# A hybrid encoder on one core: the order of every engine's instructions, written down as tables

## The chip, the core and the metric

The kernel runs on one core of one Trainium2 chip. A core has five engines that run side by side, each through its own queue in order: TensorE (PE in the profile; its weight loads are shown apart, as PEld), VectorE (DVE), ScalarE (ACT), GpSimd (POOL) and SyncE (SP). In this kernel SP issues most of the DMAs, POOL the rest, among them DMAs that add onto a tile in SBUF. An instruction that must wait for another engine holds up all that stand behind it in its own queue.

The metric is the device time of one execution in microseconds (us), the median of several runs.

## The reference

Two post-norm residual layers over 512 tokens of width 1024, in float32. Layer 0 mixes tokens by a bidirectional gated DeltaNet (8 heads of 128, a short convolution on q, k and v), layer 1 by a bidirectional GLA (4 heads, keys of 128, values of 256, a gate for each key channel). Each mixer is followed by a squared-ReLU MLP of 4096, and each of these four parts by `LayerNorm(alpha * x + part(x))`. Cut to what matters:

```python
def reference(x, ...):
    for i in range(DEPTH):                       # DEPTH = 2
        if i % 2 == 0: m = _mixer_gdn(x, ...)    # projections, conv, chunked delta rule both ways, rmsnorm * silu(z), w_out
        else:          m = _mixer_gla(x, ...)    # projections, gates, chunked GLA both ways, rmsnorm * silu(r), w_out
        x = _layernorm(DEEPNORM_ALPHA * x + m, ln1_g[i], ln1_b[i])
        a = relu(x @ mlp_w1[i])
        x = _layernorm(DEEPNORM_ALPHA * x + (a * a) @ mlp_w2[i], ln2_g[i], ln2_b[i])
    return x
```

## The kernel before

**Products in three parts.** Every large product runs on pairs of numbers in the `float32r` type: ACT rounds an operand to a high part (`nc.scalar.copy`, L104), DVE subtracts that from the operand for the low part (L105), and `mm3` (L130 to L136) issues three matmuls, high by high (L133), high by low and low by high (L135, L136). So each block of weights costs a DMA into a staging buffer (`wst`, four of them), a cast on ACT and a subtraction on DVE before PE can use it, and the staging buffer is free for the next load when both are done. The split parts go to `wh` and `wl` (three buffers each), in the MLPs also to `w2h`, `w2l` (three) and `ah`, `al` (two).

**Stages.** In the profiled execution: the DeltaNet layer from 0 to about 417 us (`gdn`), the first MLP to about 757 (`mlp`), GLA to about 976 (`gla`), and the second MLP to the end. In DeltaNet each head goes through generators (`project`, `rows`, `solve`, `recur`, `attend`, `finish`): long projections in `mm3` (PE tiles `pjq`, `pjk`, `pjv`, `pjz`), between them small fp16 groups of the triangular solve (`lv`, `hp`, `nw`) and fp32 groups of the recurrence (`m1`, `m2`, `m3`, `op`). The gates of all heads come once at the start (`gates`; `gcp` at L1492 is their cumulated sum). In the MLPs, products over half the tokens and half the depth are combined Strassen-like: `pq` (256 wide) are the first products, `pX`, `pY`, `pZ` (512 wide) the second ones, `pl` the last group. In GLA, score groups (`scp`), states (`stp`), outputs (`op`), value products (`pjv`) and the output projection (`oa`) alternate; weights of the value products are combined by adding DMAs that POOL issues (`ch<-wst`, L1068).

**What sets the order.** A scheduler (the Tile layer) orders each engine's instructions by the dependences and a priority that follows the program text; `high_priority` raises some. Inside `with c.in_order(engine)` (L61) it may not: there each instruction of that engine gets an order-only dependence on the one ahead of it in the text. This holds for PE in the start of DeltaNet, in both MLPs, in GLA and in GLA's last projection, for POOL in the MLPs and DeltaNet's constants, and for ACT in one loop of the MLPs. There the author's interleaving in the text is the order; elsewhere, and on DVE and SP throughout, it is the scheduler's.

Of the kernel before, what the change touches and what calls it, by code (L numbers as in the profile page):

```python
# [28 lines left out]
class Ctx:  # L29
# [23 lines left out]
    def after(self, ins, before):  # L53

        self.tc.add_manual_dep(
            ins.ins, before.ins.name, mybir.DependencyInfo(mybir.DependencyClass.Sync, mybir.DependencyReason.DATA),
            reason="paced")
        return ins

    @contextlib.contextmanager  # L60
    def in_order(self, engine):  # L61
# [267 lines left out]
    def out_last(self, w, ks, lhs, z, tags, par, homes=None, xtags=("tp",), late=0, room=None):  # L329

        nc = self.nc
        homes = iter(homes or [None] * len(ks))
        ws = [[self.wrows(w, k * P, hf * 512, next(homes)) for k in ks[::2]] for hf in range(2)]
        banks = {}
        self.cols = room and (par, room)

        def part(t, hf, js):
            sl = slice(t * P, (t + 1) * P)
            if (t, hf) not in banks:
                banks[t, hf] = self.bank([P, 512], F32, name="ob", tag=tags[(2 * t + hf) % len(tags)])  # L340
                if not room:
                    nc.tensor.matmul(banks[t, hf], self.ident, z[t][hf], start=True, stop=False)
            for i in js:
                ah, al = lhs(ks[i], sl)
                wh, wl = ws[hf][i // 2]
                self.mm3(banks[t, hf], ah, al, wh[:, i % 2, :], wl[:, i % 2, :], room is not None and i == 0, i == len(ks) - 1)

        n, m = len(ks), len(ks) // 2
        with self.in_order(mybir.EngineType.PE) if late else contextlib.nullcontext():
            if late:  # L350
                for t in range(2):
                    for hf in range(2):
                        part(t, hf, range(m))
            for t in range(NT):
                for hf in range(2):
                    part(t, hf, range(m if late and t < 2 else 0, n))
                    if hf == 0 and 0 < late <= t:
                        self.xpose(t - late, self.xt[t - late], xtags)
                    if room:
                        nc.vector.tensor_tensor(self.xh(t)[hf], z[t][hf], banks[t, hf], ALU.add)  # L360
                if room:
                    self.whiten(self.xh(t))
                else:
                    self.layernorm([banks[t, hf] for hf in range(2)], self.xh(t), par, last=late and t == NT - 1)
                if not late:
                    self.xpose(t, self.xt[t], xtags)
        return [t for t in range(NT - late, NT)]


def mlp(c, w1, w2, g, b, left, before=None, out=None):  # L370
# [13 lines left out]
    with c.banks(pj=2, X=2, Y=2, Z=2), tc.tile_pool(name="mlp", bufs=2) as pool:  # L384
# [372 lines left out]
        for j, t in enumerate(left):  # L757
            for q, run in enumerate(c.xposes(t, "Y", "Z")):
                between[(2, 4 * q) if j == len(left) - 1 else (0, 4 + 3 * q)] = run
        with c.in_order(mybir.EngineType.PE), c.in_order(mybir.EngineType.Pool):  # L760
            hs = {0: h}
            tail = last(G - 1, hs)
            units = seconds(hs, tail)
            halves = c.proj_halves(specs, between)
            for f, ps in enumerate(halves):
                done = act(ps, h[0][:, f, :])
                load_part(0, 0, f // 2, f % 2, done if f > 1 else None)
                if f == 0 and before:
                    lnp.extend(c.load_ln(*before, ln_tile(), acts[0]))
                    c.cols = None  # L770
            combo = combos()
            def run(n):
                for _ in range(n):
                    next(combo, None)
            op = next(combo)
            work = pairs(op, hs)
            run(3)
            w = c.wcols(w1, GF // 2 * P)
            for f in range(4, GF):
                nw = c.wcols(w1, (f + 1) * P) if f + 1 < GF else None  # L780
                run(1 if f == 6 else 2)
                done = feature(f, h, w)
                w = nw
                if f in (4, 5):
                    load_part(0, 1, 1, f % 2, done)
                if f == 5:
                    load(0, 1, 0, acts[-1])
                if f == 6:
                    next(units)
                    next(work)  # L790
            not_done.clear()
            for _ in combo:
                pass
            with c.in_order(mybir.EngineType.Activation):
                for _ in work:
                    next(units)
                next(units, None)
            par.extend(c.load_ln(g, b, ln_tile(), acts[-1]))
            for _ in tail:
                pass  # L800


def load_x(c, x, tags, zero):
    c.new_xt()
    c.new_x()
    for t in range(NT):
        c.dma(c.xt[t], x[t * P:(t + 1) * P, :])
    idle = c.bank([P, S], F32, name="idle", tag="pj")

    def warm(n=1):  # L810
        for _ in range(n):
            c.nc.tensor.matmul(idle, zero[:, 0, :], zero[:, 0:NT, :], start=True, stop=True)

    with c.in_order(mybir.EngineType.PE):
        warm(7)
        c.marks = [c.xpose(t, c.xt[t], tags, warm=warm if t < NT - 1 else None) for t in range(NT)]
    return c.marks[-1]
# [52 lines left out]
def gla(c, gc, w_in, gate_w2, w_out, cols):  # L870
# [5 lines left out]
    with c.banks(ac=2, tp=2, X=2, Y=2), tc.tile_pool(name="gla", bufs=2) as pool, \  # L876
# [11 lines left out]
        c.dma(gst, w_in[:, base:base + 32].rearrange("(k p) n -> p k n", p=P))  # L888
        specs = [(c.stack(gst, 3), "gps", "ac")]
        specs += [(c.wcols(w_in, c0), nm, "XY"[nm == "pjk"]) for c0, nm in ((0, "pjq"), (H * P, "pjk"))]  # L890
        with c.in_order(mybir.EngineType.PE):
            gps, *qk0 = c.proj_halves(specs, dict(zip(((2, 0), (2, 4)), c.xposes(NT - 1, "tp", "tp"))))
        low = slice(64, 96)
        gl3 = pool.tile([P, S], F32R, name="gl3", tag="gl3", bufs=1)
# [19 lines left out]
        lhs = lambda k, sl: tuple(t[:, k % 4, sl] for t in o_pair(k // 4))  # L914
        early = list(range(KT // 2))
        vr = GlaValues(c, pool, w_in, heads)
        with c.in_order(mybir.EngineType.PE):
            list(heads[0].qk(qk0))
            heads[0].gates(0)
            heads[0].gates(1)  # L920
            def stream():
                yield from heads[1].qk()
                yield from vr.products(0)
                yield from heads[2].qk()
                yield from vr.products(2)
                yield from heads[3].qk()
                c.new_xt()
                for t in range(NT):
                    c.dma(c.xt[t], kept[t * P:(t + 1) * P, :])
                    z.append(c.xh(t))  # L930
                yield from c.out_pieces(w_out, early, lhs, z, ("X", "Y"))

            work = stream()

            def behind(n):
                for _ in range(n):
                    next(work, None)

            spare = pool.tile([P, NT, 2 * B_DV], F32, name="vs", tag="vs", bufs=3)
            vr.first = vr.combos(spare)  # L940
            level = heads[0].levels()
            next(level)
            for _ in range(2):
                next(vr.first)
            behind(10)
            after = None
            for h in range(H):
                for s in level:
                    behind(FILL[h].get(s, 0))
                    if s == NORM_AT and after:  # L950
                        after()
                    if s in (16, 32) and h + 1 < H:
                        heads[h + 1].gates(s // 32)
                level = heads[h + 1].levels() if h + 1 < H else iter(())
                steps = iter(STEPS[h])

                def beside():
                    units, levels = next(steps)
                    behind(units)
                    for _ in range(levels):  # L960
                        next(level, None)

                heads[h].states(beside)
                after = heads[h].norm
            behind(2)
            after()
            behind(99)
# [12 lines left out]
class GlaValues:  # L980


    ORDER = (1,2,5,6,7,4,3)
# [352 lines left out]
class GdnConst:  # L1336


    def __init__(self, c, pool, pz, w_in, a_log, dt_bias, conv_w, norm_g, behind):
# [11 lines left out]
        V.memset(self.eps[:, 1:2], math.log(0.5 * P * RMS_EPS))  # L1351
        self.ng = pool.tile([P, 1], F32, name="ng", bufs=1)
        self.cw = pool.tile([P, 5, 24], F32, name="cw", bufs=1)
        with c.in_order(mybir.EngineType.Pool):
            self.gates(w_in, a_log, dt_bias, conv_w, norm_g, behind)
            self.masks()

# [63 lines left out]
    def gates(self, w_in, a_log, dt_bias, conv_w, norm_g, behind):  # L1421
# [29 lines left out]
            nc.tensor.transpose(ps[:, :120], cw, c.ident[:120, :120])  # L1451
            V.tensor_copy(self.cw, ps[:, :120].rearrange("p (k t) -> p k t", k=5))

        with c.in_order(mybir.EngineType.PE):
            ps, self.k0 = c.proj_halves([(ws, "bap", "ch"), (k0, "pjk", "ac")], {(1, 6): taps})
        yr = pool.tile([2 * M, S], F32, name="yr", tag="E", bufs=2)
        nc.scalar.copy(yr, ps[:2 * M, :])
# [501 lines left out]
        "b_gate_b", "b_norm_g", "b_w_out", "ln1_g", "ln1_b", "mlp_w1", "mlp_w2", "ln2_g", "ln2_b"]  # L1959


def body(tc, nc, a, out):
    with contextlib.ExitStack() as es:
        def pool(name, bufs, **kw):
# [4 lines left out]
        with tc.tile_pool(name="gcst", bufs=1) as gp:  # L1969
# [5 lines left out]
            left = gla(c, gc, a["b_w_in"][0], a["b_gate_w2"][0], a["b_w_out"][0], cols)  # L1975
        mlp(c, a["mlp_w1"][1], a["mlp_w2"][1], a["ln2_g"][1], a["ln2_b"][1], left,
            (a["ln1_g"][1], a["ln1_b"][1]), out=out[0])


# [16 lines left out]
```

## Time and profile before

| | |
|---|---|
| three runs | 1339.14, 1340.04, 1342.2 us; median 1340.04 |
| profiled execution | 1339.26 us, of which span 1337.6 |
| busy: PE, PEld, DVE, ACT, POOL | 1312.5, 1127.9, 1127.6, 777.7, 118.8 us |
| matmul records | 8726 |
| busy PE by stage (0:417, 417:757, 757:976, 976:1337.6) | 410.3, 338.0, 212.3, 352.0 us |

How to read it: times are microseconds from the span's start. A row of the timeline has the start, the length, the engine, the line, the operation and out<-in by the program's names, and in brackets how long the engine stood idle ahead of it and what ended that. A row of the waits names who waited for whom, then the total, the count and the longest one. The chain of waits follows the work that ended last backwards, at each step to what released it. A row by groups has the busy time and the mean in ns. Matmuls are pipelined, and the ends of their records are modelled. A row by stretch of time has, after the stretch, its length and then the busy time of PE, PEld, DVE, ACT and POOL with the number of instructions, the granted clock, the share of the DMA engines and GB/s.

### The profile page before, as it was taken

What the parts mean: (1) busy time and instruction counts of PE and PEld (TensorE: products, weight loads), DVE (VectorE), ACT (ScalarE), POOL (GpSimd) and SP (SyncE); (2) the same over time, 40 slices, a digit from 0 to 9 for tenths busy, and PEclk for the clock granted to TensorE, in tenths of its full rate; (3) what the DMA queues carried; (4) which work ended last, traced back from release to release, by engine and by line L of the source; (5) the groups of instructions that cost most, each with busy time, mean ns of one, the idle gap of its engine ahead of it and who ended that gap; (6) DMA issues with size and microseconds to landing.
All of it is one profiled execution on the core that took longest, in us unless ns stands there. A gap on an engine that the chain in (4) does not pass through costs nothing.

```text
span 1337.6 us, 22200 instructions
## 1 busy us (share of the span) xinstructions
PE 1312.5 (98%) x8726; PEld 1127.9 (84%) x8726; DVE 1127.6 (84%) x1738; ACT 777.7 (58%) x1477; POOL 118.8 (9%) x180
## 2 busy tenths in 40 slices
PE   8999999999999999999999999999999999999997
PEld 7778887888888899999998878877879899999986
DVE  6798898998768897988977889888877998889875
ACT  4766667666534656656563358647357556566640
POOL 6600000000001000101001011110000001001000
PEclk9999999999999999999999999999999999999999
DMA  7321111211133765556521666464125665556411
GB/s 196 79 64 49 49 49 48 64 46 47 52 111 110 196 135 152 130 160 160 124 83 63 183 140 158 101 152 126 44 68 156 176 173 145 139 156 129 126 63 48
DMA packets 155289, 148.86 MB, mean 111 GB/s; under 512 B 7425, under 2 KB 124193, under 8 KB 155184
## 3 DMA queue, kind: packets, MB, share of 16 engines
q1 hardware_dynamic: 144416, 115.62, 29.2%
q0 software_dynamic: 10624, 31.55, 12.6%
q8 instruction: 68, 1.11, 0.3%
q14 instruction: 37, 0.30, 0.1%
q10 hardware_dynamic: 144, 0.26, 0.1%
HBM read 118.06 MB, written 4.19 MB: 91 GB/s over the span
## 4 chain that ended last, share of the span: by engine, by line
PE 82%; DVE 7%; ACT 5%; DMA 3%; issue 2%; SPq 0%; POOL 0%; DVEq 0%; ACTq 0%; POOLq 0%
PE pq L136 6%; PE pq L133 6%; PE pq L135 6%; PE pX L135 3%; PE pX L136 3%; PE pX L133 3%; PE pjv L133 2%; PE pjv L135 2%; PE pjv L136 2%; PE pl L136 2%; PE pl L133 2%; PE pl L135 2%; PE op L1926 2%; PE lv L1789 2%; PE pY L135 2%; PE pY L136 2%
## 5 line engine op out<-in xcount | busy, mean ns | idle before, releaser
L104 ACT CAST wh<-wst 128x1024 fp32r<-128x1024 f32 (+1 forms) x175 | 173.2, 994 | 134.9 <-DVE wst L485 47.5
L105 DVE TENSOR_TENSOR wl<-wst,wh 128x1024 fp32r<-128x1024 f32 (+1 forms) x175 | 201.4, 1153 | 24.7 <-ACT wh L104 23.7
L105 DVE TENSOR_TENSOR w2l<-w2r,w2h 128x1024 fp32r<-128x1024 f32 x84 | 102.6, 1221 | 25.5 <-ACT w2h L104 25.2
L136 PE MATMUL pq<-xth,wl 128*128 128x256 f32 x384 | 108.5, 283 | 0.0
L133 PE MATMUL pq<-xth,wh 128*128 128x256 f32 x384 | 108.5, 283 | 0.0
L135 PE MATMUL pq<-xtl,wh 128*128 128x256 f32 x384 | 108.5, 283 | 0.0
L104 ACT CAST w2h<-w2r 128x1024 fp32r<-128x1024 f32 x84 | 88.1, 1049 | 5.1 <-PE pZ L136 2.6
L136 PE MATMUL pq<-t,wl 128*128 128x256 f32 x288 | 81.2, 282 | 0.4 <-DVE wl L105 0.4
L133 PE MATMUL pq<-t,wh 128*128 128x256 f32 x288 | 81.0, 281 | 0.3 <-DVE h L532 0.3
L135 PE MATMUL pq<-t,wh 128*128 128x256 f32 x288 | 81.1, 281 | 0.0
L135 PEld LDWEIGHTS pq<-xtl,wh 128*128 128x128 f32 x384 | 73.4, 191 | 3.0
L133 PEld LDWEIGHTS pq<-xth,wh 128*128 128x128 f32 x384 | 73.3, 191 | 2.9
L135 PE MATMUL pX<-w2l,ah 128*128 128x512 f32 x192 | 75.5, 393 | 0.0
L136 PE MATMUL pX<-w2h,al 128*128 128x512 f32 x192 | 75.4, 393 | 0.0
L133 PE MATMUL pX<-w2h,ah 128*128 128x512 f32 x192 | 75.1, 391 | 0.0
L136 PEld LDWEIGHTS pq<-xth,wl 128*128 128x128 f32 x384 | 73.3, 191 | 0.0
L600 POOL DMA_DIRECT2D w2r<-w2r x36 | 31.0, 877 | 404.3 <-DVE w2l L105 191.3
L485 DVE TENSOR_TENSOR wst<-wst 128x512 f32<-128x512 f32 x96 | 64.9, 684 | 0.2
L105 DVE TENSOR_TENSOR al<-h,ah 128x1024 fp32r<-128x1024 f32 x42 | 51.2, 1220 | 9.2 <-ACT ah L104 9.2
L133 PEld LDWEIGHTS pq<-t,wh 128*128 128x128 f32 x288 | 54.4, 189 | 1.6 <-DVE h L532 0.7
L135 PEld LDWEIGHTS pq<-t,wh 128*128 128x128 f32 x288 | 54.3, 188 | 1.0
L136 PEld LDWEIGHTS pq<-t,wl 128*128 128x128 f32 x288 | 54.3, 188 | 0.6 <-DVE wl L105 0.6
(557 smaller groups left out, 4049.9 us busy)
## 6 DMA issues: line engine op xcount, KB each, us to landing
wst<-in_mlp_w SPq DMA_DIRECT2D x64, 512.0 KB, 4.8
w2r<-in_mlp_w SPq DMA_DIRECT2D x64, 512.0 KB, 3.8
w2r<-w2r POOLq DMA_DIRECT2D x36, 512.0 KB, 5.6
wst<-in_a_w_in SPq DMA_DIRECT2D x32, 512.0 KB, 4.1
wst<-in_b_w_in SPq DMA_DIRECT2D x24, 256.0 KB, 3.3
wst<-in_a_w_out SPq DMA_DIRECT2D x8, 512.0 KB, 3.7
wst<-in_b_w_in SPq DMA_DIRECT2D x8, 512.0 KB, 5.5
ch<-wst POOLq DMA_DIRECT2D x8, 512.0 KB, 5.8
```

The source lines that it names most:

```text
L104: nc.scalar.copy(hi, src)
L105: self.low = nc.vector.tensor_tensor(lo, src, hi.bitcast(F32), ALU.subtract)
L133: mm(ps, ah, bh, start=start, stop=False, **kw)
L135: mm(ps, ah, bl, start=False, stop=False, **kw)
L136: mm(ps, al, bh, start=False, stop=stop, **kw)
L485: V.tensor_tensor(a, a, b, ALU.add)
L600: nc.gpsimd.dma_start(a, b, accum_op=ALU.add)
L1789: T.matmul(ps[:, u, :, :], lhs[:, u, :], cols(rhs, u, s, i), start=True, stop=True)
L1926: T.matmul(op[:, n, :], l, r, start=i == 0, stop=i == len(mm) - 1)
```

## The change

All `in_order` blocks are replaced by empty contexts. Instead, when the whole program has been traced, `written_order` reads one table for each of the five engines. A table's numbers are places in that engine's own list of instructions as the text traces them, and `a-b` is a run of them; each instruction gets an order-only dependence on the one before it in the table. The scheduler is left no choice. The tables were found by a search that used traced durations. No instruction, tile, buffer or size is changed; lines of the code behind the new function move down by 12.

```diff
+    def written_order(self, orders):
+
+        traced = list(self.nc.cur_bb.bb.instructions)
+        for name, text in orders.items():
+            own = [i for i in traced if i.engine == getattr(mybir.EngineType, name)]
+            ends = [[int(k) for k in run.split("-")] for run in text.split()]
+            seq = [own[k] for run in ends for k in range(run[0], run[-1] + 1)]
+            for prev, i in zip(seq, seq[1:]):
+                self.tc.add_manual_dep(
+                    i, prev.name, mybir.DependencyInfo(mybir.DependencyClass.NoSync, mybir.DependencyReason.DATA),
+                    reason="in_order")
...
-        with self.in_order(mybir.EngineType.PE) if late else contextlib.nullcontext():
+        with contextlib.nullcontext():
...
-        with c.in_order(mybir.EngineType.PE), c.in_order(mybir.EngineType.Pool):
+        with contextlib.nullcontext():
...
+ORDER = {
+    "PE": """
+        0-129 134-199 206-209 200-205 226-234 210-213 130-133 235-237 290-292 246-248 257-259 268-270 287-289 309-314
...
+    "SP": """
+        11-47 52-54 48-49 59-61 51 50 62-63 58 56-57 55 74-77 82-83 85 78-79 89 80 90-92 81 84 93 86-87 94 88 95-97
...
+        c.written_order(ORDER)
```

By place in their queue, 6297 of PE's 8184 instructions move, 1453 of DVE's 1740, about 1000 of ACT's 1368, 139 of SP's 252 and 41 of POOL's 185. Most move little: on average 20 places on PE (35 in the MLPs, 4 in DeltaNet, 8 in GLA), 5 on DVE, 4 on ACT, 2 on SP. In the MLPs, where PE's groups of twelve `pq` and six `pX`, `pY` or `pZ` alternated regularly, the groups are now cut into threes (one `mm3`), and `pq` mostly stands earlier, the second products later.

Three places in detail. In GLA, on ACT, at 930 to 936 us of the profile, head 2's outputs are evicted (`o`, and `op` for the sum of squares) among casts of weights; `F` is a tile that holds weights of the last output projection. Before:

```order
L1187 COPY k_10519<-pjk_10580 128x512
L1219 ACTIVATE ge_10675<-k_10519 128x512
L1310 COPY o_10642<-op_10638 128x256
L1311 ACTIVATE op_10638,ss_10630<-o_10642 128x256
L104 CAST F_11052<-wst_11050 128x1024
L1310 COPY o_10686<-op_10682 128x256
L1311 ACTIVATE op_10682,ss_10630<-o_10686 128x256
L1250 COPY sc_10674<-scp_10696 128x512
```

Now:

```order
L1322 COPY o_10642<-op_10638 128x256
L110 CAST wb_11047<-wst_11045 128x1024
L1231 ACTIVATE ge_10675<-k_10519 128x512
L1322 COPY o_10686<-op_10682 128x256
L1323 ACTIVATE op_10682,ss_10630<-o_10686 128x256
L1262 COPY sc_10674<-scp_10696 128x512
L1323 ACTIVATE op_10638,ss_10630<-o_10642 128x256
```

The cast of `F` has left this place; it now stands behind a cast that ran at 966 us.

In GLA, on DVE, at 782 to 788 us: `wl` are low parts of weights of the value products, the others update scores, gates and their operands. Before:

```order
L1245 TENSOR_TENSOR F_9220<-F_9220 128x256x2
L105 TENSOR_TENSOR wl_9365<-wst_9343,wh_9364 128x1024
L1223 TENSOR_TENSOR qh_9394<-q_9216,F_9220 128x512
L1242 TENSOR_TENSOR E_9242<-E_9242,F_9220 128x2x128x2
L1251 COPY_PREDICATED sc_9244<-mu1_1026,scp_9388 128x512
L1245 TENSOR_TENSOR F_9220<-F_9220 128x128x2x2
L105 TENSOR_TENSOR wl_9401<-wst_9346,wh_9400 128x1024
```

Now:

```order
L1257 TENSOR_TENSOR F_9220<-F_9220 128x256x2
L117 TENSOR_TENSOR wl_9365<-wst_9343,wh_9364 128x1024
L117 TENSOR_TENSOR wl_9401<-wst_9346,wh_9400 128x1024
L1238 TENSOR_TENSOR kh_9396<-k_9217,E_9242 128x512
L1024 SCALAR_TENSOR_TENSOR vs_9241<-vs_9241,xth_8684 128x1024
L1254 TENSOR_TENSOR E_9242<-E_9242,F_9220 128x2x128x2
L1235 TENSOR_TENSOR qh_9394<-q_9216,F_9220 128x512
```

`wl_9401`, the low part that ran at 786.15, follows the other `wl` at once; four updates that stood between come behind it.

At the start of DeltaNet, on PE, at 39.5 us: the four matmuls of `gcp`, between products of head 0's `pjz`. Before:

```order
L136 MATMUL pjz_522<-xth_109,wl_519 128x512
L1492 MATMUL gcp_337<-gy_313,cum0_185 128x32
L1493 MATMUL gcp_337<-gy_313,ones_187 128x32
L1492 MATMUL gcp_337<-gy_313,cum1_186 128x32
L1493 MATMUL gcp_337<-gy_313,ones_187 128x32
L133 MATMUL pjz_522<-xth_109,wh_518 128x512
```

Now:

```order
L148 MATMUL pjk_650<-xth_109,wl_647 128x512
L1664 MATMUL ktp_563<-ident_70,sil_436 128x128 x4
L1504 MATMUL gcp_337<-gy_313,cum0_185 128x32
L1505 MATMUL gcp_337<-gy_313,ones_187 128x32
L1504 MATMUL gcp_337<-gy_313,cum1_186 128x32
L1505 MATMUL gcp_337<-gy_313,ones_187 128x32
L145 MATMUL pjk_650<-xth_109,wh_646 128x512
```

The last nine matmuls of `pjz`, both groups of transposes `ktp` and nine matmuls of the next head's `pjk` have come ahead of `gcp`.

More of the change, by code (lines that the diff above doesn't have):

```diff
@@ L793, in mlp @@
                 pass
-            with c.in_order(mybir.EngineType.Activation):
+            with contextlib.nullcontext():
                 for _ in work:
@@ L812, in warm @@
             c.nc.tensor.matmul(idle, zero[:, 0, :], zero[:, 0:NT, :], start=True, stop=True)
-    with c.in_order(mybir.EngineType.PE):
+    with contextlib.nullcontext():
         warm(7)
@@ L890, in gla @@
         specs += [(c.wcols(w_in, c0), nm, "XY"[nm == "pjk"]) for c0, nm in ((0, "pjq"), (H * P, "pjk"))]
-        with c.in_order(mybir.EngineType.PE):
+        with contextlib.nullcontext():
             gps, *qk0 = c.proj_halves(specs, dict(zip(((2, 0), (2, 4)), c.xposes(NT - 1, "tp", "tp"))))
@@ L916, in gla @@
         vr = GlaValues(c, pool, w_in, heads)
-        with c.in_order(mybir.EngineType.PE):
+        with contextlib.nullcontext():
             list(heads[0].qk(qk0))
@@ L1353, in __init__ @@
         self.cw = pool.tile([P, 5, 24], F32, name="cw", bufs=1)
-        with c.in_order(mybir.EngineType.Pool):
+        with contextlib.nullcontext():
             self.gates(w_in, a_log, dt_bias, conv_w, norm_g, behind)
@@ L1452, in taps @@
             V.tensor_copy(self.cw, ps[:, :120].rearrange("p (k t) -> p k t", k=5))
-        with c.in_order(mybir.EngineType.PE):
+        with contextlib.nullcontext():
             ps, self.k0 = c.proj_halves([(ws, "bap", "ch"), (k0, "pjk", "ac")], {(1, 6): taps})
```

282 lines of the change are left out of this document (added).

## The prediction

> **What bounds the kernel now.** I read the page's first part, then busy time by stage, then what TensorE (PE) waits for, longest first.
>
> ```profile
> span 1337.6 us, 22200 instructions
> PE 1312.5 (98%) x8726; PEld 1127.9 (84%) x8726; DVE 1127.6 (84%) x1738; ACT 777.7 (58%) x1477; POOL 118.8 (9%) x180
> ```
>
> PE is busy 98% of the span. The profiled execution took 1339.26 us, 1.7 around its span; the median of the three timed runs, 1340.04, is 0.8 above it. PE is idle for 1337.6 - 1312.5 = 25.1 us in all. The next view has busy time in the DeltaNet layer (0 to 417), in the GLA layer (757 to 976), and in a steady piece of the second MLP.
>
> ```profile
> 0.00:417.00 417.00, 410.26 (x3377) 331.96 (x3378) 352.39 (x706) 252.35 (x650) 49.29 (x102) 1.00 0.26 71
> 757.00:976.00 219.00, 212.28 (x1119) 179.06 (x1118) 192.43 (x277) 133.75 (x241) 23.60 (x24) 1.00 0.52 129
> 1060.00:1160.00 100.00, 100.00 (x646) 90.95 (x645) 91.24 (x109) 61.11 (x87) 6.82 (x8) 1.00 0.57 139
> ```
>
> The columns after the length are PE, PE's weight loads, DVE, ACT, POOL and the clock. The steady piece has no idle at all, so no order can shorten it; DeltaNet has 6.7 us of idle (with the start of the program) and GLA 6.7. The clock is 1.00 throughout. PE's waits, the longest ones and those I use:
>
> ```profile
> PE gcp L1492 <- DVE gy L1487: 1.6, 1, 1.6
> PE otp L1326 <- DVE o L1322: 1.5, 2, 1.3
> ...
> PE scp L1212 <- ACT op L1311: 1.4, 1, 1.4
> PE pjv L135 <- DVE wl L105: 1.2, 2, 0.8
> PE tp L195 <- DVE xt L289: 1.1, 1, 1.1
> PE stp L1292 <- ACT st L1295: 1.1, 1, 1.1
> PE pj L136 <- DVE al L105: 0.7, 1, 0.7
> ...
> PE pjv L133 <- ACT wh L104: 0.4, 1, 0.4
> ...
> PE kdp L1280 <- DVE ge L1269: 0.4, 1, 0.4
> PE pq L136 <- DVE wl L105: 0.4, 1, 0.4
> PE pj L135 <- DVE xtl L208: 0.3, 1, 0.3
> PE op L1308 <- ACT sc L1250: 0.3, 1, 0.3
> PE pq L133 <- DVE h L532: 0.3, 1, 0.3
> PE op L1308 <- DVE st L1298: 0.3, 1, 0.3
> PE pj L133 <- ACT xth L207: 0.2, 1, 0.2
> ```
>
> So the kernel is bound by the amount of PE work, with some twenty single waits on top. Each wait costs more than its idle time says, because a matmul's modelled end lies behind the start of the next one:
>
> ```profile
> 1063.24 0.40 PE L135 MATMUL pZ<-w2l,ah 128*128 128x512 f32 x1
> 1063.47 0.40 PE L136 MATMUL pZ<-w2h,al 128*128 128x512 f32 x1
> ```
>
> Starts are 0.23 apart while a record is 0.40 long, so the first 0.16 us or so of a wait is hidden in the record ahead of it. I add 0.16 to each wait.
>
> [...]
>
> **The change part by part.** No instruction is added, removed or resized; 8726 matmul records, the DMAs and the ACT table loads are the same. What changes is who stands behind whom. I followed each wait above through the two orders.
>
> *ACT, 936 (scp, 1.4).* PE waits for ACT's `op` and `o` evictions, which stand behind a cast whose operand is still in a DMA:
>
> ```profile
> 934.54 1.04 ACT L104 CAST F<-wst 128x1024 fp32r<-128x1024 f32 x1 [2.07 <-DMA wst<-in_b_w_out]
> 935.49 0.36 ACT L1310 COPY o<-op 128x256 f32<-128x256 f32 x1
> 935.89 0.39 ACT L1311 ACTIVATE op<-o 128x256 f32<-128x256 f32 x1
> ```
>
> ACT stands 2.07 us and then casts for 1.04. The table moves the cast some 30 us down, so `o` and `op` come 3 us sooner and the wait goes: 1.4 + 0.16. The cast's staging buffer comes free later, and SP holds the load into it, with all of SP behind: loads of the second MLP's first weights, first used at 1003 or later, which is slack enough.
>
> *ACT, 872 (stp, 1.1).* The same pattern:
>
> ```profile
> 872.02 1.04 ACT L104 CAST wh<-ch 128x1024 fp32r<-128x1024 f32 x1 [2.57 <-DMA ch<-wst]
> 873.29 0.64 ACT L1295 COPY st<-stp 128x256 f32<-128x256 f32 x2
> ```
>
> Now `st` stands ahead of the cast, and on DVE its next two `st` updates stand ahead of `wl` (op, 0.3). The other `op` wait (0.3) has more PE groups ahead of it. Together 1.7 + 3 x 0.16 = 2.2.
>
> *DVE, 787 to 806 (pjv, 1.2 + 0.4).* The chain of waits goes through two DMAs:
>
> ```profile
> 785.56 0.68 DVE F L1245
> 786.24 1.15 DVE wl L105
> ...
> 787.85 3.54 DMA wst<-in_b_w_in
> ...
> 792.90 6.67 DMA ch<-wst
> ...
> 800.74 1.22 DVE wl L105
> ```
>
> The `wl` at 786.24 frees a staging buffer; the load into it and then POOL's accumulating DMA wait for it. Its cast, the second of these two, had ended at 782.94:
>
> ```profile
> 780.75 2.19 ACT L104 CAST wh<-wst 128x1024 fp32r<-128x1024 f32 x2
> ```
>
> but four updates (`qh`, `E`, `sc`, `F`, some 0.6 each by the 0.68 of `F`) stand between. The table puts `wl` ahead of them: the chain starts about 2.5 us sooner, more than the three waits: 1.6 + 3 x 0.16 = 2.1. The four updates come 1.2 us later; the `scp` groups that use them are later in PE's table too.
>
> *DVE, 949 (otp, 1.5).* Two small steps of an rsqrt and four products `o` stood among five updates of some 0.6; two of these move out, 1.2 us. PE's transposes also get a score group ahead of them. 1.5 + 2 x 0.16 = 1.8.
>
> *PE, 39.5 (gcp, 1.6).* Four tiny matmuls wait for a chain of DVE steps on the gates. They move behind 18 matmuls of 0.23 and two groups of transposes of some 0.44, 5 us; DVE's chain is put back by two convolution steps (1.5 us). The wait goes: 1.6 + 0.16. Its results feed the rows of head 0, which both orders have well behind this place.
>
> *PE elsewhere.* Ahead of the transposes at 755.8 (tp, 1.1) stand more matmuls of the next projection: I count 9 of some 0.12, 1.1 us, so nearly all of 1.3 goes, 1.1 taken. `pq` at 1054 and 1056 (0.3 + 0.4) get nine 512-wide matmuls ahead of them, 2 us: 0.7 + 0.32 = 1.0. `pj` at 1002 and 1003 (0.2 + 0.3) get about 15 of 0.12, and DVE's `xtl` moves ahead of a `wl` of 1.2: 0.5 + 0.32 = 0.8. `kdp` (0.4) has its `ge` ahead of a `wl`: 0.6. The start of the program and `al` (0.7) stand where they stood: 0.
>
> *Change of kind.* A 512-wide product that follows the fp16 groups of DeltaNet's solve starts its successor later:
>
> ```profile
> 242.02 0.40 PE L133 MATMUL pjk<-xth,wh 128*128 128x512 f32 x1
> 242.26 0.39 PE L135 MATMUL pjk<-xtl,wh 128*128 128x512 f32 x1
> ...
> 243.20 0.47 PE L133 MATMUL pjk<-xth,wh 128*128 128x512 f32 x1
> 243.51 0.39 PE L135 MATMUL pjk<-xtl,wh 128*128 128x512 f32 x1
> ```
>
> 0.31 against 0.24: 0.07 to 0.08 each. In the two orders I count 105 such changes before and 87 now: 18 x 0.08 = 1.4. In the MLPs changes between 256- and 512-wide groups rise from 198 to 358; at such a change (1063.47 and its neighbours follow one) I see no extra, so 0.
>
> *DeltaNet's short waits* under 0.16 us are in no row. By the bound of 0.16 and two such places in each of eight heads they are between 0 and 2.6; the table moves most instructions there by few places; I take 1.0.
>
> Sum: 1.6 + 2.2 + 2.1 + 1.8 + 1.8 + 1.1 + 1.0 + 0.8 + 0.6 + 1.4 + 1.0 = 15.4. In the other direction the new orders make waits that no trace shows. Their bounds are 0 (every producer still comes ahead) and, if as many new waits of the mean size come as go, some 13, which takes all back but the changes of kind. I take 0, the nearer row being the steady piece with no idle, and carry the rest in the rivals. 1339.3 - 15.4 = 1323.9, and 0.8 more by the median is 1324.7: **1324 us**, own range 1319 to 1330.
>
> **The rivals.**
>
> *Half the gain.* GLA's chain is two DMAs (3.54 and 6.67) in a row, and DVE is busy 192.4 of 219 us there. If these set the pace, not the place of one `wl`, the waits of `pjv`, `stp`, `op` and `kdp` come back elsewhere: 2.1 + 2.2 + 0.6 = 4.9, and with the two small terms gone (2.4) 1324 + 7.3 = 1331. For it speaks DVE's 88%; against it that each of those waits was traced to one instruction in the wrong place.
>
> *The full gain.* Waits that I left (`al`, short ones, the rest at 755) go as well, 0.9 + 1.6 + 0.2, and DeltaNet's visits get cheaper in all kinds, not fp16 alone. The first matmul of a product shows what is there:
>
> ```profile
> L133 PE MATMUL pjz<-xth,wh 128*128 128x512 f32 x64 | 29.2, 456 | 0.0
> L135 PE MATMUL pjz<-xtl,wh 128*128 128x512 f32 x64 | 25.1, 392 | 0.0
> ```
>
> 64 ns x 64 for `pjz`, and about as much for `pjk`, `pjq` and `pjv`, is 16 us; a third of it gives 5. 1324 - 2.7 - 5 = 1316.
>
> *Slower: the MLPs' second products fall behind.* The table lets first products (`pq`) run ahead and delays `pX`, `pY`, `pZ` and the splits of their weights, 84 in a ring of three pairs.
>
> ```profile
> L104 ACT CAST w2h<-w2r 128x1024 fp32r<-128x1024 f32 x84 | 88.1, 1049 | 5.1 <-PE pZ L136 2.6 <-DMA w2r<-in_mlp_w 2.3
> ```
>
> A cast of `w2h` whose buffer is still being read stands at the head of ACT's queue, and `wh` for the next `pq` stands behind it; with PE's order fixed nothing else can run. One such case costs up to a cast and a subtraction, 1.05 + 1.22 (the `wl` at 800.74) = 2.3 us. From (15.4 + 2.7) / 2.3 = 8 of the 84 on the kernel is slower; at twelve it takes 1324 + 27.6, about 1352. Against it: ACT waits for PE's last product only 2.6 us over all 84 today, and is 61% busy in the steady piece. For it: nearly two thousand of each MLP's some 2100 matmuls change place, where there was little to win.
>
> *No change.* New waits take all 13 back: 1337 to 1342.
>
> *Packed to the weight loads.* If a new order could overlap matmuls until weight loads filled PE, the span would be 1127.9 and the 25.1 of idle, about 1155 in all. The even starts of 0.23 under loads of 91% speak against it. [...]
>
> **How the numbers follow.** The forecast 0.40; half the gain 0.18; the full gain 0.20; no change 0.07; slower 0.14; packed 0.01. About 0.2%, 2.7 us, is what a measurement can tell from no change, so 1337.4 to 1342.7 is the same. Faster is 0.40 + 0.18 + 0.20 + 0.01 = 0.79, same 0.07, slower 0.14. The range of 1309 to 1341 leaves out the slower case, the packed one, and a few hundredths at the low end of the full gain and the high end of no change.
>
> **What would show it.** In the changed kernel's waits of PE, `gcp`, `scp`, `stp` and `otp` should be gone or under 0.3, and `pjv` under 0.5; ACT's cast of `F` should show no idle ahead of `o`. GLA's 219 us should be about 8 shorter with PE idle under 3. DeltaNet should end about 4 sooner. A steady MLP stretch must still be all busy; if PE shows waits for `wl`, `w2l` or `h` there, the slower rival is at work. A gain that sits inside the MLPs would prove the reading of the bound wrong.

## The result and the profile after

The changed kernel takes 1325.86 us, the median of five runs (1325.09 to 1326.56), against 1339.82 before: a ratio of 0.9893, 95% interval 0.988 to 0.9907, so 1.07% faster; the two medians are 14.0 us apart. The forecast was 1324. The profiled execution went from 1339.26 to 1325.86.

The changed kernel's page, first part:

```profile
span 1323.8 us, 22196 instructions
PE 1307.9 (99%) x8726; PEld 1131.5 (85%) x8726; DVE 1137.1 (86%) x1738; ACT 773.8 (58%) x1477; POOL 120.3 (9%) x180
```

Busy time by stretch (the columns as before), with the four stages at their new bounds and the same steady piece of the second MLP:

```profile
0.00:416.00 416.00, 410.48 (x3377) 335.44 (x3378) 355.16 (x706) 252.34 (x650) 51.15 (x102) 1.00 0.25 71
754.00:963.00 209.00, 208.32 (x1115) 178.88 (x1115) 192.13 (x277) 133.01 (x236) 24.03 (x24) 1.00 0.54 137
...
1070.00:1170.00 100.00, 100.00 (x648) 91.19 (x647) 90.19 (x109) 61.85 (x92) 6.01 (x7) 1.00 0.55 143
```

GLA is 10 us shorter between these bounds, with 0.7 us of PE idle where there were 6.7. DeltaNet has 5.5 us of idle against 6.7. The steady piece is as it was: all busy.

PE's waits, the longest ones:

```profile
PE bap L166 <- DVE ws L160: 1.6, 1, 1.6
PE idle L824 <- DVE pz L1521: 1.5, 1, 1.5
PE pq L145 <- DVE h L564: 1.2, 1, 1.2
PE pq L145 <- ACT h L555: 0.8, 1, 0.8
PE ktp L1664 <- ACT sil L1647: 0.6, 1, 0.6
PE ktp L1664 <- ACT sil L1643: 0.4, 1, 0.4
PE lv L1801 <- ACT pz L1821: 0.4, 1, 0.4
```

`gcp`, `scp`, `otp`, `pjv`, `tp` at 755, both `pj` and the stop of 1.1 at `stp` are gone. Two of `pq` have come, and longer ones of `ktp` and `lv` than before.

For a sharper account I took the time from each matmul's start to the next one's, and added it up by the stage that the matmul belongs to. It holds what a wait hides in the record ahead. Where a single wait is given as "late" below, it is such a start-to-start time less what the same kinds of neighbours take elsewhere.

| start-to-start, us | before | changed | changed, second profile |
|---|---|---|---|
| DeltaNet | 416.1 | 415.1 | 415.1 |
| first MLP | 339.1 | 337.6 | 337.6 |
| GLA | 219.0 | 210.2 | 210.7 |
| second MLP | 353.1 | 351.0 | 350.9 |

So 8.3 to 8.8 us come from GLA, 3.6 from the MLPs, and 1.0 from DeltaNet. Four kernels below have this order of GLA, too, and take 211.2 to 211.7 us there; over all these executions GLA's gain is 7.3 to 8.8.

### The profile page after: what moved, and what is told of

Its sections match the earlier page's. It is cut to its first block, busy times and chain, and to the rows that moved or that the text cites. A ratio compares the mean times of both kernels' runs of the same rounds, so it can differ in the third digit from the quotient of the medians.

```text
span 1323.8 us, 22196 instructions
## 1 busy us (share of the span) xinstructions
PE 1307.9 (99%) x8726; PEld 1131.5 (85%) x8726; DVE 1137.1 (86%) x1738; ACT 773.8 (58%) x1477; POOL 120.3 (9%) x180
## 4 chain that ended last, share of the span: by engine, by line
PE 91%; ACT 4%; DVE 3%; issue 1%; DMA 1%; DVEq 0%; ACTq 0%
PE pq L145 6%; PE pq L148 6%; PE pq L147 6%; PE pX L147 3%; PE pX L148 3%; PE pX L145 3%; PE pjv L145 3%; PE pjv L148 3%; PE pjv L147 3%; PE pj L147 2%; PE pj L145 2%; PE pj L148 2%; PE pl L147 2%; PE pl L145 2%; PE pl L148 2%; PE op L1938 2%
## 5 line engine op out<-in xcount | busy, mean ns | idle before, releaser
L116 ACT CAST w2h<-w2r 128x1024 fp32r<-128x1024 f32 x84 | 87.8, 1050 | 31.8 <-issue 8.3
L116 ACT CAST ah<-h 128x1024 fp32r<-128x1024 f32 x42 | 44.1, 1050 | 24.5 <-PE pX L147 15.4
```

The source lines that it names most:

```text
L116: nc.scalar.copy(hi, src)
```

## Experiments

All kernels here are the changed kernel with other tables; the rest of the code is the same. A kernel "before" some time and "changed" after it has each engine's queue pieced together from the two orders at that time of their profiles. Names in the diffs are instructions of one engine's queue, in order. Times of before in the three jobs: 1339.88, 1340.21 and 1340.68 us.

### GLA's order alone

```diff
 every engine's table:
   up to 757 us of before:  the order of before
-  GLA:                     the order of before
+  GLA:                     the new order (up to 963 us of its profile)
   from there to the end:   the order of before
```

> The new order from 757 us to the end of GLA alone, on all five engines; everywhere else the order of the kernel before. My theory (each stage's gain is its own single waits): the stage's start-to-start time falls from 219.0 to about 210.2 us as in the changed kernel, the other stages keep theirs, so 1339.8 - 8.7 = 1331.1 us. Rival (GLA's gain needs the changed MLP ahead of it, which hands it its operands sooner): half of it or less, 1335.5 or more.

Measured 1331.53 us (ratio 0.9939, 0.9926 to 0.9951), GLA 211.2 us, the other stages within 0.5 of before. The stage's gain is its own and adds to the others'; the rival falls.

### DeltaNet back in the order of before

```diff
 every engine's table:
-  up to 417 us:            the new order
+  up to 417 us:            the order of before
   from there to the end:   the new order
```

> The changed kernel with DeltaNet (0 to 417 us) put back into the order of before. By the prediction's terms for DeltaNet (gcp 1.8, change of kind 1.4, short waits 1.0) it should lose 4.2 us: 1325.9 + 4.2 = 1330.1. By the two traces (416.08 against 415.13 us of starts) it loses 1.0: 1326.8, and the table gives nearly all of its 4.2 back in new waits.

Measured 1327.68 us (0.9913, 0.9899 to 0.9926), with DeltaNet at 415.7. DeltaNet's table, over three thousand matmuls long, is worth 0.5 us by the stage, and by the totals between 0.6 (the changed kernel run again, below) and 1.8. The predicted 4.2 isn't there.

### Ten instructions moved in the order of before

```diff
 PE, 37 us:      pjz_522 (last before the stop)
-                gcp x4
                 pjz_522 x9
+                gcp x4
 DVE, 782 us:    wl_9365
+                wl_9401
                 qh_9394  E_9242  sc_9244  F_9220
-                wl_9401
 ACT, 872 us:    -wh_10156 (from here)     +wh_10156 behind st0_10171, st1_10175
 DVE, 873 us:    -wl_10157 (from here)     +wl_10157 behind the four st updates
 ACT, 934 us:    -F_11052 (from here)      +F_11052 behind the cast at 966
 DVE, 946 us:    -qh_10821, xt2 (from here) +both behind the four o products
```

> The order of before with nine instructions moved at five places: gcp's four matmuls behind nine of pjz (1.8), DVE's wl at 786 us ahead of four updates (2.1), ACT's wh cast at 872 and its wl behind the st evictions and updates (1.7: stp and one op), ACT's F cast at 934 behind the cast at 966 (1.6), two DVE updates at 946 behind the four o products (1.2). My theory (each wait is one instruction in the wrong place): 1339.8 - 8.4 = 1331.4 us and the five waits gone or under 0.3. Rival (the pace of GLA's DMAs and of DVE sets the time, not places): the GLA waits come back behind the places, only gcp, F and o gain, 1335 or more. No gain at all would mean that only the orders as a whole work.

Counted one by one the edit moves ten instructions, not nine: `gcp`'s four and six more. Measured 1333.69 us (0.9956, 0.9943 to 0.9968): 6.2 of the 8.4 us. DeltaNet gained 1.4 of `gcp`'s 1.8, GLA 4.2 of 6.6. PE's waits in GLA now:

```profile
PE op L1320 <- ACT sc L1262: 0.7, 1, 0.7
...
PE otp L1338 <- DVE o L1334: 0.5, 2, 0.3
...
PE pjv L147 <- DVE wl L117: 0.4, 1, 0.4
...
PE stp L1304 <- ACT kdt L1294: 0.3, 1, 0.3
...
PE scp L1224 <- DVE qh L1235: 0.2, 1, 0.2
```

The long stops are gone, and pieces of them stand at the neighbours: `op` waits for `sc`, `stp` now for `kdt`, `scp` for `qh`. In GLA 13 places were more than 0.14 late before, 8.9 us together; 12 are here, 4.8 together; 4 in the changed kernel, 1.3 together. Each long stop went at its own place, so the misplaced instruction is its cause; the moves were made in one kernel, and what each is worth alone isn't shown. Together they bring three quarters of their terms, and in GLA two thirds. The rest, and the small stops that I had not counted, seem to need the neighbours moved too. `gcp`'s move alone gains as much in DeltaNet as the whole table does (414.7 against 414.6 to 415.1 in the kernels with the table's order there).

### The changed kernel with two evictions moved

Its two new waits in the MLPs have the old pattern. DVE at 1050 us, and ACT at 690, in the changed kernel:

```profile
1047.90 0.43 DVE L561 SCALAR_TENSOR_TENSOR h<-pq,h 128x256 f32<-128x256 f32 x1 [0.24 <-PE pq L148]
1050.34 0.69 DVE L497 TENSOR_TENSOR wst<-wst 128x512 f32<-128x512 f32 x1 [2.01 <-DMA wst<-in_mlp_w]
1050.95 1.22 DVE L622 TENSOR_TENSOR h<-h 128x1024 f32<-128x1024 f32 x1
1052.08 0.41 DVE L564 SCALAR_TENSOR_TENSOR h<-h,pq 128x256 f32<-128x256 f32 x1
```

```profile
688.70 1.05 ACT L116 CAST w2h<-w2r 128x1024 fp32r<-128x1024 f32 x1 [0.51 <-PE pY L148]
689.65 1.04 ACT L694 CAST wh<-w2r 128x1024 fp32r<-128x1024 f32 x1
690.60 0.41 ACT L571 ACTIVATE h<-h 128x256 f32<-128x256 f32 x1
690.91 0.35 ACT L555 COPY h<-pq 128x256 f32<-128x256 f32 x1
```

DVE stands 2.01 us for a DMA with the eviction that PE needs (L564) two places behind. ACT's cast of `w2h` stands for `pY`, which still reads its buffer, and the eviction (L555) is behind that.

```diff
 DVE:  h_11818 (L561)
+      h_11818 (L564)
       wst_11781 (L497)   h (L622)
-      h_11818 (L564)
 ACT:  w2h
+      h<-pq (L555)
       wh   h (L571)
-      h<-pq (L555)
```

> The changed kernel with two instructions moved, at its two new waits in the MLPs: on DVE at 1050 us the eviction h (from pq) ahead of an update that stands 2.0 us for a DMA, on ACT at 690 us the eviction of pq ahead of a cast and a square. If the two waits are single instructions in the wrong place, pq's waits of 1.2 and 0.8 us go with their hidden parts (1.42 and 0.95 of start-to-start time): 1325.9 - 2.4 = 1323.5 us. If they are slack that the MLP needs elsewhere, 1325.9, and another wait shows up within the next 20 us.

Measured 1324.54 us (0.9886, 0.9873 to 0.99), and both waits are gone. The MLPs are 0.8 and 0.8 shorter, 1.6 of 2.4: again two thirds. In this execution `pjv` waits at 800 us (0.4) where the profile of the changed kernel has none; the last run comes back to that.

### A group of matmuls ahead of each place that still waits

```diff
 PE, at ktp, rtp, ktp, lv, ktp, lv, lv, lv, otp, tp, pjv, kdp, stp:
+      the next three 512-wide matmuls of the queue
       the waiting group
-      the three
 (with the two moves above)
```

> The changed kernel with both moves of the run before it (the two evictions in the MLPs) and, on TensorE, one group of three 512-wide matmuls brought ahead of each of thirteen places that still wait (ktp, rtp, lv, otp, tp in DeltaNet; pjv, kdp, stp in GLA), each of which waits 0.28 to 0.74 us of start-to-start time, 6.1 us in all. If each place is slack that a 0.7 us group fills at no price, 1324.5 - 6.1 = 1318.4 us. From the moves in the order of before, of which two thirds to three quarters of the sum stayed, some 4: 1320.5. If the waits only walk on to the next place, 1324.5.

Measured 1327.48 us (0.9905, 0.9892 to 0.9919), against 1324.54 (0.9886) without them. DeltaNet kept 0.2 of the 4.7 us of its ten places (414.3 against 414.6): its waits walked on to the next `ktp`, `lv` and `tp`. GLA lost 2.9. PE at 912 us, and busy time there:

```profile
912.54 0.40 PE L145 MATMUL oa<-wh,oth 128*128 128x512 f32 x1
915.37 0.50 PE L147 MATMUL oa<-wl,oth 128*128 128x512 f32 x1 [2.44 <-DVE wl L117]
...
917.29 3.12 PE L1224 MATMUL scp<-qh,kh 128*128 128x128 f32 x16
```

```profile
912.70:915.30 2.60, 0.24 (x1) 0.00 (x0) 2.60 (x5) 0.71 (x1) 0.94 (x1) 1.00 0.00 0
915.30:917.50 2.20, 2.13 (x11) 1.99 (x12) 1.16 (x2) 0.00 (x0) 0.00 (x0) 0.73 0.41 82
917.50:920.00 2.50, 2.50 (x14) 2.50 (x14) 0.76 (x1) 1.65 (x5) 0.00 (x0) 0.55 0.86 297
```

The group of `oa` that I brought ahead of `kdp` has weights that aren't there yet: 2.6 us late. And behind the stop the granted clock falls from 1.00. The trace's records of the clock have 0.50 from 916.32 to 919.74; the last two rows mix that with 1.00. In these 3.4 us the matmuls of `kdp` and `scp` follow each other by 0.213 us instead of 0.11, which costs another 1.6 us. My rule (what follows in the queue is ready) failed at one place of thirteen, and that took more than the others gave.

### The second MLP's body back in the order of before

```diff
 every engine's table:
   up to 1062 us:           the new order
-  from there to the end:   the new order
+  from there to the end:   the order of before
```

> The changed kernel up to 1062 us, the order of before from there to the end: the body of the second MLP, where most matmuls of the table have changed place. The prediction's reading (a steady stretch is all busy, no order can shorten it): 1325.9 us within 1, and the body's start-to-start time the same. The slower rival's reading (the table's late second products cost something there) would give less than 1325; a gain of the table inside the body would give 1327 or more.

Measured 1328.6 us (0.991, 0.9896 to 0.9923); the second MLP takes 352.7. Of the 1.7 above the changed kernel 1.5 is one wait 3.6 us behind the seam of the two orders:

```profile
1065.62 0.50 PE L148 MATMUL pY<-w2h,al 128*128 128x512 f32 x1 [1.34 <-DVE al L117]
```

Its steady piece is as busy as the others:

```profile
1070.00:1170.00 100.00, 100.00 (x647) 90.84 (x646) 89.36 (x109) 62.82 (x89) 5.13 (x6) 1.00 0.60 154
```

So the body in the one order and in the other differs by 0.2. That the wait comes from the seam alone isn't shown, but neither parent order has it. By the total the kernel misses the 1326.9 that I allowed; 1.5 is the seam, and GLA, which is the same in both, was 211.7 in this execution.

### What a change of kind costs

```diff
 PE, 38 places in DeltaNet:
       first half of a run of fp16 matmuls
+      three 512-wide products
       second half
-      three 512-wide products
```

> The order of before with 38 runs of fp16 matmuls in DeltaNet's solve cut in two, a group of three 512-wide products between the halves: 38 more changes from fp16 to a 512-wide product, nothing else. At 0.085 us each (0.314 against 0.229) 3.2 us: 1339.9 + 3.2 = 1343.1, and a little more where a half that comes 0.7 us later is waited for. If a change of kind costs nothing of itself, 1339.9.

Measured 1347.26 us (1.0054, 1.0039 to 1.007): 7.1 slower. By the rows the starts of the changed kinds take 3.6 more, or 0.096 a place. Another 1.6 of the 9 us in DeltaNet aren't the edit's: in the profiled execution the clock was 0.50 from 41.94 to 45.35, behind `gcp`'s stop, and the first moved instruction stands at 67 us (the last section comes back to this). The rest are mostly waits: places that are over 0.14 late grew from 16 to 35 and from 8.5 to 14.2 us, of which six places and 1.2 us lie in that stretch. A half run of the solve that comes 0.7 us later is waited for in many places.

> The same with 65 runs of float32 matmuls and transposes in DeltaNet and GLA, cut in two by three 512-wide products. As the prediction has it every change of kind into a 512-wide product costs 0.08: 1339.9 + 5.2 = 1345.1. By the rows of both kernels the last float32 matmul or transpose of a run is followed 0.081 sooner than one within it, which takes the 0.085 back: 1339.9 + 0.3, and what the later halves are waited for.

The same edit at 65 runs of float32 matmuls and transposes in DeltaNet and GLA: 1344.12 us (1.0035, 1.0019 to 1.0052). By the rows the changes themselves cost nothing in DeltaNet and 0.4 in GLA. Of the 3.6 by which DeltaNet grew in the profiled execution, 1.5 is again a stretch at half clock, from 14.36 to 17.77 and so ahead of the first edit at 25 us; the rest are waits. Why these changes are free is to be seen in the profile of before, at the end of a group of transposes:

```profile
42.57 0.60 PE L1652 MATMUL ktp<-ident,sil 128*128 128x128 f32 x4
42.92 0.48 PE L133 MATMUL pjk<-xth,wh 128*128 128x512 f32 x1
43.24 0.39 PE L135 MATMUL pjk<-xtl,wh 128*128 128x512 f32 x1
```

Four transposes of 0.109 would last 0.44; the product behind them starts after 0.35, and takes 0.32 to its successor instead of 0.23. Its extra is the 0.08 that the last transpose didn't take. The last of a run of 64-wide fp16 matmuls takes 0.029 like the others, so there nothing is given back.

### Two instructions put back in the changed kernel

```diff
 ACT, 926 us:  wb   ge
+              F_11052
               o_10686   op_10682
-              F_11052 (from 957 us)
 DVE, 781 us:  wl_9365
-              wl_9401
               kh  vs  E_9242  qh_9394
+              wl_9401
```

> The changed kernel with two instructions put back where the order of before had them: ACT's F cast ahead of o and op at 926 us, DVE's wl at 781 behind four updates. By the prediction's terms: scp waits again, 1.6, and pjv 2.1: 1325.9 + 3.7 = 1329.6. If the pace of the two DMAs sets pjv and not wl's place, its part is 1.0 or less: 1328.5 or less. If the rest of the table has made room for both, 1325.9.

Measured 1333.35 us (0.9945, 0.9931 to 0.9959), 6.2 above the changed kernel in the same job, where the terms said 3.7. `scp` waits again (0.78 late). `pjv` is 4.6 late at three places, more than the 2.3 of before:

```profile
796.94 1.06 PE L1224 MATMUL scp<-qh,kh 128*128 128x128 f32 x8
800.54 0.50 PE L145 MATMUL pjv<-wh,cb 128*128 128x512 f32 x1 [2.55 <-ACT wh L116]
801.80 0.50 PE L147 MATMUL pjv<-wl,cb 128*128 128x512 f32 x1 [0.76 <-DVE wl L117]
...
803.10 0.63 PE L145 MATMUL pjv<-wh,cb 128*128 128x512 f32 x1
803.53 0.63 PE L147 MATMUL pjv<-wl,cb 128*128 128x512 f32 x1
```

```profile
800.50:802.50 2.00, 1.20 (x4) 0.79 (x5) 1.82 (x2) 0.49 (x1) 0.46 (x1) 1.00 0.46 86
802.50:805.00 2.50, 2.50 (x8) 1.68 (x6) 0.44 (x1) 1.52 (x2) 2.01 (x2) 0.50 0.39 44
```

The second of the two adding transfers that `pjv` waits for was issued 39.0 us behind the stage's start; before it was 37.7, in the changed kernel 35.2. So the chain through `wl` came out longer than before, which the terms did not hold: from the start of the load to the issue of the first adding transfer 7.0 us pass, before 5.1, and nearly all of the difference is the load itself, 5.43 us against 3.54. Why it is slower isn't settled. Again the granted clock is 0.50 behind a stop of 2.55 us: five products at 0.43 instead of 0.23, another 1.0. So these two instructions, with what followed from them, hold 6 of the 14 us.

### The changed kernel again, and a better version

> The changed kernel once more, unchanged, in the same job as the two others, so that differences of 0.1% between them can be read: 1325.9 us. In four other kernels with the same order of GLA the weights of pjv at 800 us came 0.4 to 0.8 us late, in the profile of the changed kernel not at all. If that profile was one lucky execution, pjv waits here; if the move of wl cures it, it does not.

Measured 1327.12 us (0.9898, 0.9884 to 0.9911), and `pjv` waits 0.2 (0.32 late). The weights come by two adding DMAs that POOL issues, each with a cast on ACT that waits for it. In the changed kernel's first profile, and in the kernel with ten moves:

```profile
787.88 1.18 POOL L1080 DMA_DIRECT2D ch<-wst  x1
789.53 0.85 POOL L1080 DMA_DIRECT2D ch<-wst  x1 [0.47 <-DVE wl L117]
...
794.66 1.05 ACT L116 CAST wh<-ch 128x1024 fp32r<-128x1024 f32 x1 [6.68 <-DMA ch<-wst]
797.61 1.05 ACT L116 CAST wh<-ch 128x1024 fp32r<-128x1024 f32 x1 [0.53 <-DMA ch<-wst]
```

```profile
789.90 0.94 POOL L1080 DMA_DIRECT2D ch<-wst  x1
793.45 0.85 POOL L1080 DMA_DIRECT2D ch<-wst  x1 [2.61 <-DVE wl L117]
...
796.61 1.05 ACT L116 CAST wh<-ch 128x1024 fp32r<-128x1024 f32 x1 [6.86 <-DMA ch<-wst]
799.46 1.05 ACT L116 CAST wh<-ch 128x1024 fp32r<-128x1024 f32 x1 [0.85 <-DMA ch<-wst]
```

From its issue to its cast the first takes 6.8 and 6.7 us. The second is there 2.95 and 2.85 us behind the first, though it was issued 1.65 behind in the one and 3.55 behind in the other. So moving `wl` up gains until the second transfer stands right behind the first, and leaves a rest. In the six profiles with this order up to there `pjv` is 0, 0.32, 0.55, 0.73, 1.00 and 1.30 us late near 800 us: that the changed kernel's first profile had no such wait was luck.

> The changed kernel with the two evictions of the MLPs moved as before, and of the thirteen moves on TensorE only three: pjv at 800 us (0.55 there in the run with the two evictions), otp at 399 (0.40) and tp at 415 (0.74). The trio of oa that stood 2.4 us for its weights stays where the changed kernel has it. If that trio and the lower clock behind it made the run of thirteen slow, 1324.5 less what the three give, two thirds of 1.7: 1323.4, and the clock 1.00 at 915 to 920. If the moves themselves cost, 1325 or more.

```diff
 the two evictions moved as above, and on PE
+  three 512-wide matmuls ahead of pjv at 800, otp at 399, tp at 415
```

Measured 1324.51 us (0.9879, 0.9866 to 0.9893), 2.6 below the changed kernel in the same job (1323.9 to 1324.95 against 1326.11 to 1327.59). It beats both kernels, but with 1324.54 for two moves the three more matmul groups give nothing that can be measured: `pjv` is still 0.29 late, and the wait of `tp` at 415 is 0.57 late at the next `tp`, 421. Without the group of `oa` there is no long stop at 915, and the clock is 1.00 there; so that group, with the low clock behind it, made the run of thirteen slow.

## Why the prediction was right, and where not

**The bound.** Right. PE's work sets the time: the steady piece is all busy in either order, the second MLP's body is worth 0.2, and the gain sits where single waits were. The 0.16 us that a record hides held as well: `gcp`'s idle of 1.59 was 1.75 late, `scp`'s 1.4 was 1.56, `otp`'s 1.3 was 1.49.

**GLA.** The terms `scp` 1.6, `stp` and `op` 2.2, `pjv` 2.1, `otp` 1.8 and `kdp` 0.6 make 8.3; the stage gained 7.3 to 8.8, by the execution. ACT now evicts `o` and `op` with no idle between, and `F` is gone from there:

```profile
924.39 0.37 ACT L1322 COPY o<-op 128x256 f32<-128x256 f32 x1 [2.98 <-PE op L1320]
924.66 1.05 ACT L110 CAST wb<-wst 128x1024 fp32r<-128x1024 f32 x1
...
926.14 0.36 ACT L1322 COPY o<-op 128x256 f32<-128x256 f32 x1
926.54 0.39 ACT L1323 ACTIVATE op<-o 128x256 f32<-128x256 f32 x1
```

The idle of 2.98 is for PE now and no longer for a DMA. Term by term it was less exact than the sum: the ten moves alone gave two thirds of their terms in GLA, and the rest of the stage's gain is in small stops that I had no rows for. `kdp` and `stp` still wait at 914 and 918 (0.50 and 0.45 late).

**`pjv` and the DMAs.** The mechanism was right: put back, the wait returns. "The chain starts about 2.5 us sooner, more than the three waits" took the durations of the DMAs as fixed. But the second of the two adding transfers comes 2.5 to 4.1 us behind the first, with its issue anywhere between 0.5 and 3.55 us behind. The rival of half the gain, that the DMAs' pace and not a place sets this, was right for a part: up to 1.3 us of the 2.3 by which `pjv` was late before.

**DeltaNet.** Wrong: 4.2 forecast, 1.0 in the two profiles, 0.5 by the kernel with this stage put back. Three steps failed. *Change of kind* (1.4): I counted fp16 runs ahead of 512-wide products alone, 105 to 87. Both profiles have these counts, so 1.4 was saved there; but runs of fp16 ahead of float32 matmuls, whose first one takes 0.08 longer too, rose from 16 to 36, 1.6 lost. Of the term nothing is left. *New waits* ("I take 0", and the bound of 13 left to the rivals): eight places with `ktp`, `lv` and `rtp` are now 0.29 to 0.72 late, 3.5 us in all, against `gcp`'s 1.8 that went. *Short waits* (1.0): they were there, eleven places with `ktp` and `lv` that were 0.15 to 0.37 late before, 2.5 us together, and nearly all have gone; but the eight new ones took more than that back. The nearer row for the new waits was not the steady piece of an MLP but the solve itself, where half a run that comes 0.7 us later is waited for.

**The MLPs.** The terms `tp` 1.1, `pj` 0.8 and `pq` 1.0 make 2.9; the two stages gained 3.6. The waits named are gone, but two of `pq` have come (1.42 and 0.95 late). What covered them is `al` at 430, which I had left standing (0.83 late before, gone now), and stops too small for the list.

**The total.** That it came within 2 us is in part luck. DeltaNet's terms were 3.2 too high; the MLPs gave 0.7 more than theirs, and the profiles by which I read the result are those in which GLA came out best.

**The slower rival.** Its mechanism is there, once: the cast of `w2h` at 688.70, which stands for `pY` with an eviction behind it. It needed 8 of 84 such cases. The other new wait for `h`, at 1052, is behind an update that stands for a DMA.

**What would show it.** `gcp`, `scp`, `otp` gone, `stp` 0.3, `pjv` under 0.5 in both profiles of the changed kernel, GLA 8 shorter with idle under 3, the MLPs' steady stretch all busy: all came. "DeltaNet should end about 4 sooner" did not.

## What to carry to other kernels

In a kernel whose matmul engine is nearly always busy, look for the few instructions in the wrong place, above all those that stand for a DMA with an eviction behind them: ten moved instructions gave 6.2 of 14 us, two put back took 6. Bringing work forward to fill a stop is safe only where its operands' arrival has been read from the trace, since one group brought ahead of its weights cost more than the twelve others gave. A stage that is a tight chain (here the triangular solve) gives little to a reordering, so count new waits there, and not only the ones that go.

## What the runs showed of the hardware

**Behind some stops the granted clock fell from 1.00 to 0.50, and a stop's length alone doesn't tell which.** Four of the thirteen profiles have a granted clock of 0.50 between the first matmuls and the last, each time for 3.41 us: behind stops of 2.44 and 2.55 us in the two kernels above, and in the two kernels with split runs, ahead of any edit, behind `gcp`'s stop of 1.58 and behind one of `bap` of 1.99 at 13 us (first row: split fp16 runs; second: split float32 runs):

```profile
41.94:45.35 3.41, 3.41 (x11) 2.72 (x10) 1.67 (x3) 1.88 (x3) 0.00 (x0) 0.50 0.03 6
```

```profile
14.36:17.77 3.41, 3.41 (x19) 3.33 (x17) 0.26 (x1) 1.15 (x2) 2.96 (x13) 0.50 1.05 265
```

Before, the same stops (1.59 for `gcp`, 1.99 for `bap`) left the clock at 1.00. Behind `gcp`:

```profile
39.50:42.00 2.50, 2.48 (x15) 2.24 (x16) 1.36 (x6) 1.67 (x3) 0.00 (x0) 1.00 0.79 211
```

What decides isn't shown. Behind the stops of 2.44 and 2.55 us the drop came 0.95 us (915.37 to 916.32) and about 2.0 us (800.54 to 802.5) after PE went on. A wait's price isn't linear in these runs: in the kernel with thirteen groups 2.6 us late cost 4.2, and the stops of 1.58 and 1.99 us cost 1.6 and 1.5 more in the two profiles with split runs and nothing in that of before.

**A change to 512-wide products costs time behind fp16, but not behind float32.** 38 more changes from fp16 to 512-wide products cost 3.6 us of starts, 65 from float32 or transposes 0.4: the last of those is followed 0.08 sooner, which makes up for the slower start of the product.

**The second of two adding transfers.** Of the two 512 KB transfers `ch<-wst` the first takes 6.7 to 7.3 us from issue to cast in all thirteen profiles. The second comes 2.5 to 4.1 us behind the first, with its issue anywhere between 0.5 and 3.55 us behind, so it takes 6.0 us at the widest spacing and up to 10.3 at the closest. What sets the 2.5 to 4.1 isn't shown.
